# An encoder layer on one core: folded softmax sums, another load order and another place for the layer norm's root

## The chip, the cores and the metric

The kernel runs on one core of one Trainium2 chip. A core has five engines with queues of their own: TensorE (PE in the profile, PEld for its weight loads), VectorE (DVE), ScalarE (ACT), GpSimd (POOL) and SyncE (SP), which only issues DMAs here. The metric is the device time of one execution in microseconds (us). Times inside an execution count from the start of its profiled span.

## The reference

One encoder layer on 2048 tokens of width 1024. A projection of `x` feeds two groups of heads: gated linear attention (group A) and softmax attention with compressed queries and keys (group B). Their outputs stand side by side, go through one output projection, and a residual with layer norm follows. What the change touches:

```python
# group B: 4 heads, blocks of queries
s = einsum('bqhd,bkhd->bhqk', qn, k_nope) + einsum('bqhr,bkr->bhqk', qr, k_r)
p = softmax(s, axis=-1)
o_b = einsum('bhqk,bkhv->bqhv', p, v) * silu(gate)
# both groups
mixed = concatenate([o_a, o_b], axis=-1) @ w_out
# layer norm of the residual
r = DEEPNORM_ALPHA * x + mixed
mu, var = mean(r), mean((r - mu) ** 2)          # along the width of 1024
out = (r - mu) * rsqrt(var + 1e-5) * ln_g + ln_b
```

All tensors are float32. The kernel splits each operand of a product into a high and a low part and multiplies three times (`mm3`, L417: lines L419 to L421), so that the faster matmul format keeps enough digits.

## The kernel before

Two sweeps over chunks of 128 tokens make the projections and group A and leave the compressed keys, values and rotary keys of group B on the chip. Then comes `attention` (L1499), which holds both the softmax attention and the output stage.

**Attention.** There are 16 blocks (`nb`): for each of four query blocks of 512 columns, four heads. A block has eight steps (`NP`) of two key tiles each. Scores stand with keys on the partitions and the 512 queries along the free axis. One step issues ten score matmuls (`scores`), a copy to SBUF on ACT (`copy`, L1542), maxima on DVE (`smax`, L1555); once the block's maximum is known (`tmax`, `rmax`, `bmax`: transposes, a reduce, transposes back) a subtraction on DVE (`sub`, L1579), the exponential (`exp`, L1583) and the high part (`phi`) on ACT, the low part on POOL (`plo`, L371) and six matmuls with the values (`pv`).

The denominators are sums of the exponentials over all keys. DVE adds four of the eight steps in a PSUM bank `ap` (`acc0` on ACT copies the first half step, L1598; `acc`, L1606), POOL adds the other four into an SBUF tile `as` of two halves (printed as `acc`). `tot` joins them: `ap` plus one half, then that plus the other half, into SBUF (L1629, L1630). `tsum` turns the 128x512 sum with four transposes (L1642), `rcp` reduces over the 128 partial sums and takes reciprocals (L1648, L1649), a column of 128x4. `keep` (L1654) stores it from ACT's queue, in 512 pieces of four bytes, into `r_s`, from where the output stage reads it along rows. For the last block `turn` transposes the column to 4x128 instead and `rows` (L1666, L1667) copies it on ACT and stores it from SP's queue. `oh` and `ol` split the block's output on ACT and DVE, `y` multiplies it by the value weights, `yc` copies and stores it (L1689, L1690).

**Order.** Each of these steps has a place, in units of a step (`PLACE`, L74; for the last block `PLACE_LAST`, L96; for what is already of the output stage `PLACE_OUT`, L107). A list of all steps sorted by place fixes the order of the instructions on every engine, SP's queue included (L1761). The place of a step is its block's first step plus what the table says; `tot` and what follows it count from the block's last step (L1726). Tiles of the pools `pX` (tag `x`) and `pA` (tag `ap`), each one PSUM bank, and the tile `as` have one buffer: who writes the next waits for all who used the last.

**Output stage.** `OutProj` works through 16 chunks of 128 tokens. `load` (L1863 to L1866) brings a chunk of both groups' outputs (`of`) and of gate and reciprocals (`gr`), `gate` (L1872, POOL) multiplies, `hi` and `lo` split on ACT and POOL, `load_res` (L1885) brings the residual `xr` into one of three buffers. `part` multiplies one eighth of the width for the two halves of the columns. Weight blocks come through `fetch_w` (L1829), which has one buffer, and `split_hi`, `split_lo`. `residual` adds `xr` on DVE (L1939) and collects statistics (L1940); `finish` (L1942) makes mean and variance, subtracts and scales (L1951), takes the root and writes (L1954, L1955). The root is `rsqrt` (L444): logarithm and exponential on ACT (L432, L433) for a first value, one Newton step in four small DVE operations (L438 to L441).

Chunks 0 to 3 start within the sorted list. For chunks 4 to 15 (L1799) the order is written out for ACT, POOL and SP only: splits of chunk c+2, loads of chunk c+4, residual load of chunk c+1, product, finish. In that loop chunk 4 also issues `keep` of block 14 and the last block's `tot`, `oh`, `ol`; chunk 5 its `tsum` and `rcp`; chunk 7 `turn`, `y`, `rows`, `yc`. Even chunks from 2 on use the banks `mb` and `x` (`pmb`, `px` in the profile), the others a pair of banks `pS` (`po`).

Of the kernel before, what the change touches and what calls it, by code (L numbers as in the profile page):

```python
# [9 lines left out]
F32 = mybir.dt.float32  # L10
F32R = mybir.dt.float32r
I32 = mybir.dt.int32
AF = mybir.ActivationFunctionType
ALU = mybir.AluOpType
AX = mybir.AxisListType
# [3 lines left out]
P = 128  # L19
# [3 lines left out]
NCH = S // P  # L23
# [4 lines left out]
QB = 512  # L28
# [56 lines left out]
    rmax=1.27,  # L85
    bmax=1.48,
    tot=11.2,
    tsum=12.04,
    rcp=13.55,
    keep=14.21,  # L90
    oh=12.34,
    ol=12.99,
    y=16.55,
    yc=16.9,
# [20 lines left out]
    w_hi=0.74,  # L115
    w_step=6.49,
    w_lo=4.26,
    part=(1.05, 2.03, 5.45, 8.05, 10.24, 17.37, 21.96, 27.24),
    whole=(24.99, 55.73),
    sum=(38.16, 49.19),  # L120
# [234 lines left out]
class K:  # L355
# [80 lines left out]
    def rsqrt_b(self, u, y, t, w, r):  # L436
# [3 lines left out]
        nc.vector.tensor_scalar(t, w, -0.5, 1.5, ALU.mult, ALU.add)  # L440
        nc.vector.tensor_tensor(r, t, y, ALU.mult)  # L441
        return r

    def rsqrt(self, pool, u, n, name):  # L444
        return self.rsqrt_b(*self.rsqrt_a(pool, u, n, name))


    def load_w(self, pool, stage, src, ncols, tag, k, lo_eng="dve", hi_eng="act", bufs=None):
# [1050 lines left out]
    def attention(self):  # L1499
        tc, nc = self.tc, self.nc  # L1500
        mm = nc.tensor.matmul
        V, G, Ac = nc.vector, nc.gpsimd, nc.scalar
        NP = NKT // 2
        with ExitStack() as ctx:
# [4 lines left out]
            pM, pO, pX, pA, pS = bank("pM"), bank("pO"), bank("pX"), bank("pA"), bank("pS", 2)  # L1509
            blocks = [(h, b) for b in range(NQB) for h in range(H)]  # L1510
            nb = len(blocks)
            stt = [dict(s=[None] * NP) for _ in blocks]
# [110 lines left out]
            def tot(i):  # L1623
                d = stt[i]
                if i == nb - 1:
                    d["as"] = self.keep.tile([P, 2, QB], F32, tag="acc", name=f"acc{i}")
                    V.tensor_copy(d["as"][:, 0], d["ap"])
                    return
                V.tensor_tensor(d["ap"], d["ap"], d["as"][:, 1], ALU.add)  # L1629
                V.tensor_tensor(d["as"][:, 0], d["ap"], d["as"][:, 0], ALU.add)  # L1630

            def close(i, shape, name, other):


                p, tag = other if i == nb - 1 else (pX, "x")
                return p.tile(shape, F32, tag=tag, name=name)

            def tsum(i):
                d = stt[i]
                d["x"] = close(i, [P, 4, P], f"sx{i}", (pA, "ap"))  # L1640
                for e in range(4):
                    nc.tensor.transpose(d["x"][:, e], d["as"][:, 0, e * P:(e + 1) * P], self.ident)  # L1642

            def rcp(i):

                d = stt[i]
                rc = op.sm.tile([P, 4], F32, tag="rc", name=f"rc{i}")
                V.tensor_reduce(rc, d["x"], AX.X, ALU.add)  # L1648
                V.reciprocal(rc, rc)  # L1649
                d["rc"] = rc  # L1650

            def keep(i):
                h, b = blocks[i]
                Ac.dma_start(self.r_s[b][:, h].rearrange("o (e p) -> p (o e)", p=P), stt[i]["rc"])  # L1654

            def turn(i):

                d = stt[i]
                t = pA.tile([P, QB], F32, tag="ap", name=f"rt{i}")
                nc.tensor.transpose(t[0:4, 0:P], d["rc"], self.ident)  # L1660
                d["rt"] = t[0:4, 0:P]

# [38 lines left out]
            op = OutProj(self, ctx, qp, bp, sp, pS, pM, pX, pO, pA)  # L1701
            first = [dict(c=c) for c in range(4)]
# [4 lines left out]
            def put(place, fn, *a):  # L1707
                todo.append((place, len(todo), fn, a))

            def at(f, i, j=None):  # L1710
                p = PLACE_LAST.get(f, PLACE[f]) if i == nb - 1 else PLACE[f]
                return p[j] if isinstance(p, tuple) else p

            own = (("tot", tot), ("tsum", tsum), ("rcp", rcp), ("keep", keep), ("oh", oh), ("ol", ol), ("y", y), ("yc", yc))
            own_late = tuple(e for e in own if e[1] is not keep)
            for i in range(nb):
                for j in range(NP):
                    t = NP * i + j
# [11 lines left out]
            out = PLACE_OUT  # L1730
            end = NP * nb
            for k in range(NK):
                if k < PRE_W:
                    v = NP * (PRE_BLOCK + k)
                    hi, lo = v + out["pre_hi"], v + out["pre_lo"]
                else:
                    hi = end + out["w_hi"] + (k - PRE_W) * out["w_step"]
                    lo = hi + out["w_lo"]
                if k == 0:
                    put(hi - 6, op.fetch_w, k)  # L1740
                put(hi, op.split_hi, k)
                put(lo, op.split_lo, k)
                if k + 1 < NK:
                    put(lo + 0.01, op.fetch_w, k + 1)
                else:
                    put(max(lo, end + 26) + 0.02, op.load_ln)
                put(end + out["part"][k], lambda k: [op.part(o, k) for o in first[:2]], k)
            for c, o in enumerate(first):
                put(end + (out["lo1"][c - 1] + 0.01 if c else out["hi0"][0] - 6), op.load, o)
                for j in range(2):  # L1750
# [16 lines left out]
            rest = {c: o for c, o in enumerate(first)}  # L1767

            def load(c):
                if c < NCH:  # L1770
                    rest[c] = dict(c=c)
                    op.load(rest[c])

            def split(c):
                if c < NCH:
                    op.hi(rest[c], 0)
                    op.lo(rest[c], 0)
                    op.gate(rest[c])
                    op.hi(rest[c], 1)
                    op.lo(rest[c], 1)  # L1780
# [17 lines left out]
                    op.finish(rest[c])  # L1798
            for c in range(4, NCH):  # L1799
                with fixed():  # L1800
                    split(c + 2)
                    load(c + 4)
                    if 4 < c < NCH - 1:
                        op.load_res(rest[c + 1])
                    op.product(rest[c])
                    op.finish(rest[c])
                with self.after(*last.values()), fixed():
                    if c == 4:
                        keep(nb - 2)
                    for f in {4: (tot, oh, ol), 5: (tsum, rcp), 7: (turn, y, rows, yc)}.get(c, ()):  # L1810
                        f(nb - 1)


class OutProj:
# [127 lines left out]
    def finish(self, o):  # L1942
        kern, nc, sm = self.k, self.nc, self.sm
        V, Ac = nc.vector, nc.scalar
        c, rr = o["c"], o["rr"]
        mv = sm.tile([P, 2], F32, tag="mv", name=f"mv{c}")
        u = sm.tile([P, 1], F32, tag="u", name=f"u{c}")
        V.bn_aggr(mv, o["bn"])
        V.tensor_scalar(u, mv[:, 1:2], LN_EPS, None, ALU.add)
        for n in range(2):  # L1950
            V.scalar_tensor_tensor(rr[:, n], rr[:, n], mv[:, 0:1], self.ln[0][:, n], ALU.subtract, ALU.mult)  # L1951
        rs = kern.rsqrt(sm, u, 1, f"ln{c}")
        for n in range(2):
            V.scalar_tensor_tensor(rr[:, n], rr[:, n], rs, self.ln[1][:, n], ALU.mult, ALU.add)  # L1954
            nc.sync.dma_start(kern.out[c * P:(c + 1) * P, n * 512:(n + 1) * 512], rr[:, n])  # L1955
# [68 lines left out]
```

## Time and profile before

| | us |
|---|---|
| median of 3 runs | 1300.88 |
| lowest and highest | 1297.87, 1301.57 |
| profiled execution | 1303.84 |
| its span | 1301.6 |
| mean granted TensorE clock | 0.996 of full speed |

Attention runs from about 627 us to 1110, the output stage from there to the end; the two overlap for some 20 us. A row of a timeline has start, duration, engine, line, operation, `out<-in` by the program's names, shape and count; in brackets stands how long the engine had been idle and what released it. Operations of one kind that follow each other are merged into one row.

### The profile page before, as it was taken

How to read it: one execution, taken by the hardware profiler on the slowest of the kernel's cores; microseconds unless marked ns; L12 is line 12 of the kernel's file. 1: busy time of each engine (PE TensorE's matmuls, PEld its weight loads, DVE VectorE, ACT ScalarE, POOL GpSimd, SP SyncE). 2: the span in 40 equal slices, each digit the busy share in tenths (PEclk: the TensorE clock that was granted, in tenths of full speed). 3: DMA queues.
4: the chain of work that ended last, by engine and by line, in shares of the span. 5: the costliest groups of instructions: out<-in, count | busy, mean ns of one | idle time of the engine just before them, and what ended most of it. 6: DMA issues, size and time to landing. Idle time of an engine off the chain costs nothing.

```text
span 1301.6 us, 19963 instructions
## 1 busy us (share of the span) xinstructions
PE 1273.0 (98%) x7017; PEld 1122.8 (86%) x7017; DVE 927.6 (71%) x1712; ACT 817.4 (63%) x1387; POOL 785.4 (60%) x500
## 2 busy tenths in 40 slices
PE   7999999999999999999999999999999999998997
PEld 7999999999889999999788888888888888886886
DVE  6865664545665555555888888888888888386998
ACT  7765556565676566555788887888888887411110
POOL 0244232332567666661398888889999999934441
PEclk9999999999999999999999999999999999999999
DMA  8232222131566555656301112212233110376563
GB/s 288 72 90 66 81 66 81 53 94 53 200 203 192 187 179 200 206 179 203 96 1 41 42 41 50 52 46 57 57 89 90 41 41 25 121 241 163 189 203 102
DMA packets 113964, 145.82 MB, mean 112 GB/s; under 512 B 18018, under 2 KB 70630, under 8 KB 113864
## 3 DMA queue, kind: packets, MB, share of 16 engines
q1 hardware_dynamic: 105176, 142.41, 35.6%
q0 software_dynamic: 768, 2.10, 0.4%
q8 instruction: 56, 0.92, 0.3%
q10 hardware_dynamic: 7920, 0.03, 0.3%
q14 instruction: 44, 0.36, 0.1%
HBM read 94.14 MB, written 50.36 MB: 111 GB/s over the span
## 4 chain that ended last, share of the span: by engine, by line
PE 83%; DMA 4%; DVE 3%; ACT 3%; POOL 2%; issue 2%; SPq 0%; DVEq 0%; POOLq 0%; ACTq 0%
PE o L419 4%; PE o L420 4%; PE pS L1533 4%; PE o L421 4%; PE pS L1535 4%; PE pS L1536 4%; PE pS L1537 4%; PE pS L1534 4%; PE ipa L419 4%; PE ipa L421 3%; PE ipa L420 3%; PE pz L420 2%; PE pz L419 2%; PE pz L421 2%; PE ipg L419 2%; PE ipg L420 2%
## 5 line engine op out<-in xcount | busy, mean ns | idle before, releaser
L371 POOL TENSOR_TENSOR pl<-s,ph 128x1024 fp32r<-128x1024 f32 x128 | 306.4, 2413 | 58.4 <-ACT ph L365 54.6
L1555 DVE TENSOR_TENSOR rm<-pS,rm 128x512 f32<-128x512 f32 x210 | 144.9, 690 | 36.6 <-ACT s L1542 31.5
L1542 ACT ACTIVATE s<-pS 128x1024 f32<-128x1024 f32 x128 | 131.5, 1027 | 60.8 <-PE pS L1537 52.3
L1579 DVE TENSOR_TENSOR s<-s,mb 128x1024 f32<-128x1024 f32 x128 | 151.2, 1213 | 9.1 <-PE mb L1573 9.0
L1042 POOL TENSOR_TENSOR Us<-Us,cw 128x512 f32<-128x512 f32 x16 | 18.6, 1162 | 212.4 <-DVE Us L1040 180.7
L365 ACT ACTIVATE ph<-s 128x1024 fp32r<-128x1024 f32 x128 | 135.1, 1057 | 17.1 <-PE o L421 16.6
L1583 ACT ACTIVATE s<-s 128x1024 f32<-128x1024 f32 x128 | 131.4, 1050 | 13.4 <-DVE s L1579 13.3
L419 PE MATMUL ipa<-wah,xah 128*128 128x384 f32 (+1 forms) x384 | 131.2, 342 | 6.9 <-ACT wah L365 6.4
L420 PE MATMUL ipa<-wal,xah 128*128 128x384 f32 (+1 forms) x384 | 125.5, 327 | 0.1
L421 PE MATMUL ipa<-wah,xal 128*128 128x384 f32 (+1 forms) x384 | 124.8, 325 | 0.0
L1533 PE MATMUL pS<-qh,ckvT_h 128*128 128x512 f32 x256 | 102.5, 400 | 0.8 <-ACT s L1583 0.4
L419 PE MATMUL o<-ph,vh 128*128 128x512 f32 x256 | 101.0, 395 | 0.0
L421 PE MATMUL o<-ph,vl 128*128 128x512 f32 x256 | 99.8, 390 | 0.0
L1536 PE MATMUL pS<-rh,krs 128*128 128x512 f32 x256 | 99.8, 390 | 0.0
L1535 PE MATMUL pS<-qh,ckvT_l 128*128 128x512 f32 x256 | 99.8, 390 | 0.0
L1537 PE MATMUL pS<-rl,krs 128*128 128x512 f32 x256 | 99.7, 389 | 0.0
L1534 PE MATMUL pS<-ql,ckvT_h 128*128 128x512 f32 x256 | 99.7, 389 | 0.0
L420 PE MATMUL o<-pl,vh 128*128 128x512 f32 x256 | 99.7, 389 | 0.0
L371 POOL TENSOR_TENSOR ol<-of,oh 128x512 fp32r<-128x512 f32 x32 | 42.9, 1343 | 70.4 <-ACT oh L365 69.6
L1606 DVE TENSOR_TENSOR ap<-ap,s 128x512 f32<-128x512 f32 x120 | 83.1, 692 | 2.6 <-ACT s L1583 0.7
L419 PEld LDWEIGHTS ipa<-wah,xah 128*128 128x128 f32 x384 | 72.9, 190 | 9.9 <-ACT wah L365 6.6
L419 PE MATMUL pz<-xch,wzh 128*128 128x256 f32 x256 | 74.8, 292 | 0.0
(325 smaller groups left out, 3825.2 us busy)
## 6 DMA issues: line engine op xcount, KB each, us to landing
xcf<-xT_dram SPq DMA_DIRECT2D x16, 512.0 KB, 4.5
xr<-x_dram SPq DMA_DIRECT2D x16, 512.0 KB, 5.7
out_dram<-rr SPq DMA_DIRECT2D x32, 256.0 KB, 2.4
xaf<-xT_dram SPq DMA_DIRECT2D x14, 512.0 KB, 3.8
oib<-oi_s SPq DMA_DIRECT2D x16, 256.0 KB, 3.9
qdb<-qd_s SPq DMA_DIRECT2D x16, 256.0 KB, 5.0
SU<-su_s SPq DMA_DIRECT2D x16, 256.0 KB, 4.4
ub<-u_s SPq DMA_DIRECT2D x16, 256.0 KB, 4.2
```

What stands on the lines that cost most here:

```text
L365: return nc.scalar.activation(dst, src, AF.Copy).ins
L371: return e.tensor_tensor(dst, src, hi.bitcast(F32), ALU.subtract).ins
L419: mm(out, ah, bh, start=start, stop=False)
L420: mm(out, ah, bl, start=False, stop=False)
L421: mm(out, al, bh, start=False, stop=stop)
L1533: mm(ps[:, e], kh, qh, start=True, stop=False)
L1534: mm(ps[:, e], kh, ql, start=False, stop=False)
L1535: mm(ps[:, e], kl, qh, start=False, stop=False)
L1536: mm(ps[:, e], kr, rh, start=False, stop=False)
L1537: mm(ps[:, e], kr, rl, start=False, stop=True)
L1555: V.tensor_tensor(d["rm"], src[:, e], d["rm"], ALU.max)
L1579: V.tensor_tensor(s, s, d["mb"][:, None, :].to_broadcast([P, 2, QB]), ALU.subtract)
```

## The change

It makes five edits.

1. **Folded sum, blocks 0 to 14.** `tot` adds both halves of `as` into the PSUM bank. Two ACT copies (`own_half`) take, of query columns 0 to 255, the sums on partitions 0 to 63, and of columns 256 to 511 those on partitions 64 to 127, into one 128x256 tile. Two DVE additions (`fold`) add what stands on the other 64 partitions. `tsum` then needs two transposes and `rcp` reduces 64 sums for each query instead of 128. Block 15 keeps the old way.
2. **Block 14's reciprocals.** `keep` in the output stage is gone. `turn` (in bank `pX`) and `rows` of block 14 stand in the sorted list at 13.6 and 13.65, after its `rcp`.
3. **First products of the output stage.** Chunk 0's first `part` moves ahead of the last block's `tmax` (place 0.255 past the end instead of 1.05); chunk 1's stays.
4. **Load order.** From chunk 5 on `load_res` of the next chunk is issued ahead of the splits and the four loads.
5. **The layer norm's root.** The four small DVE operations become four ACT copies with factor and addend.

```diff
 PLACE = dict(
     tot=11.2,
-    tsum=12.04,
+    half=11.7,
+    fold=11.95,
+    tsum=12.37,
     rcp=13.55,
     keep=14.21,
+    turn=13.6,
+    rows=13.65,
...
 PLACE_OUT = dict(
+    part0=(0.255, 1.05),
     part=(1.05, 2.03, 5.45, 8.05, 10.24, 17.37, 21.96, 27.24),
...
             def tot(i):
...
-                V.tensor_tensor(d["ap"], d["ap"], d["as"][:, 1], ALU.add)
-                V.tensor_tensor(d["as"][:, 0], d["ap"], d["as"][:, 0], ALU.add)
+                for e in range(2):
+                    V.tensor_tensor(d["ap"], d["ap"], d["as"][:, e], ALU.add)
+
+            halves = [(slice(64 * e, 64 * e + 64), slice(64 - 64 * e, 128 - 64 * e), slice(e * QB // 2, (e + 1) * QB // 2))
+                      for e in range(2)]
+
+            def own_half(i):
+                d = stt[i]
+                for own_p, _, qs in halves:
+                    Ac.activation(d["as"][own_p, 0, :QB // 2], d["ap"][own_p, qs], AF.Copy)
+
+            def fold(i):
+                d = stt[i]
+                for own_p, other_p, qs in halves:
+                    h = d["as"][own_p, 0, :QB // 2]
+                    V.tensor_tensor(h, d["ap"][other_p, qs], h, ALU.add)
...
             def tsum(i):
-                for e in range(4):
+                for e in range(4 if i == nb - 1 else 2):
                     nc.tensor.transpose(d["x"][:, e], d["as"][:, 0, e * P:(e + 1) * P], self.ident)
...
             def rcp(i):
-                V.tensor_reduce(rc, d["x"], AX.X, ALU.add)
+                if i == nb - 1:
+                    V.tensor_reduce(rc, d["x"], AX.X, ALU.add)
+                else:
+                    V.tensor_reduce(rc.rearrange("p (e j) -> p j e", e=2),
+                                    d["x"][:, 0:2].rearrange("p j (e k) -> p j e k", e=2), AX.X, ALU.add)
...
             def turn(i):
-                t = pA.tile([P, QB], F32, tag="ap", name=f"rt{i}")
+                t = (pA if i == nb - 1 else pX).tile([P, QB], F32, tag="ap" if i == nb - 1 else "x", name=f"rt{i}")
...
-            own = (("tot", tot), ("tsum", tsum), ("rcp", rcp), ("keep", keep), ("oh", oh), ("ol", ol), ("y", y), ("yc", yc))
-            own_late = tuple(e for e in own if e[1] is not keep)
+            own = (("tot", tot), ("half", own_half), ("fold", fold), ("tsum", tsum), ("rcp", rcp), ("keep", keep), ("oh", oh), ("ol", ol), ("y", y), ("yc", yc))
+            own_late = tuple(e for e in own if e[1] is not keep) + (("turn", turn), ("rows", rows))
...
-                put(end + out["part"][k], lambda k: [op.part(o, k) for o in first[:2]], k)
+                for o, place in zip(first, out["part0"]):
+                    put(end + (out["part"][k] if k else place), op.part, o, k)
...
             for c in range(4, NCH):
                 with fixed():
+                    if 4 < c < NCH - 1:
+                        op.load_res(rest[c + 1])
                     split(c + 2)
                     load(c + 4)
-                    if 4 < c < NCH - 1:
-                        op.load_res(rest[c + 1])
                     op.product(rest[c])
                     op.finish(rest[c])
                 with self.after(*last.values()), fixed():
-                    if c == 4:
-                        keep(nb - 2)
...
     def finish(self, o):
-        rs = kern.rsqrt(sm, u, 1, f"ln{c}")
+        l, y, t, w, rs = (sm.tile([P, 1], F32, tag=f"rs_{i}", name=f"ln{c}_{i}") for i in "lytwr")
+        Ac.activation(l, u, AF.Ln)
+        Ac.activation(y, l, AF.Exp, scale=-0.5)
+        Ac.activation(t, y, AF.Copy, scale=y)
+        Ac.activation(w, t, AF.Copy, scale=u)
+        Ac.activation(t, w, AF.Copy, scale=-0.5, bias=1.5)
+        Ac.activation(rs, t, AF.Copy, scale=y)
```

More of the change, by code (lines that the diff above doesn't have):

```diff
@@ L442, in rsqrt_b @@
         return r
-    def rsqrt(self, pool, u, n, name):
-        return self.rsqrt_b(*self.rsqrt_a(pool, u, n, name))
     def load_w(self, pool, stage, src, ncols, tag, k, lo_eng="dve", hi_eng="act", bufs=None):
```

## The prediction

> **What bounds the kernel now.** I read the page's busy times first, then the busy time by stretches for attention and output, then the timelines of TensorE (PE), VectorE (DVE), ScalarE (ACT), GpSimd (POOL) and SyncE's queue (SP) where PE stands still. The stretches' columns are length, busy time and count of PE, weight load, DVE, ACT and POOL, granted clock, DMA share, GB/s.
>
> ```profile
> PE 1273.0 (98%) x7017; PEld 1122.8 (86%) x7017; DVE 927.6 (71%) x1712; ACT 817.4 (63%) x1387; POOL 785.4 (60%) x500
> 627.00:1090.00 463.00, 461.07 (x2116) 380.81 (x2115) 402.61 (x535) 381.85 (x410) 406.87 (x177) 1.00 0.18 48
> 1190.00:1210.00 20.00, 14.72 (x58) 11.59 (x57) 8.23 (x14) 2.19 (x5) 7.79 (x7) 0.83 0.83 239
> 1230.00:1250.00 20.00, 20.00 (x90) 16.57 (x89) 19.55 (x28) 3.13 (x8) 9.22 (x8) 1.00 0.66 205
> ```
>
> PE is full almost everywhere: 461 of 463 us in attention, 20 of 20 in the settled output stage, where DVE (19.55) is close behind. So an edit is worth what it takes from PE's own work or from PE's pauses. The one large pause lies between 1190 and 1210, and the clock falls there too.
>
> **The folded sum, on PE.**
>
> ```profile
> 950.47 0.39 PE L1537 MATMUL pS<-rl,krs 128*128 128x512 f32 x1
> 950.70 0.60 PE L1642 MATMUL sx<-ident,acc 128*128 128x128 f32 x4
> 951.37 0.39 PE L1534 MATMUL pS<-ql,ckvT_h 128*128 128x512 f32 x1
> 954.78 0.39 PE L1533 MATMUL pS<-qh,ckvT_h 128*128 128x512 f32 x1
> ```
>
> A 128x512 matmul takes 0.23 of PE's time (950.47 to 950.70). The four transposes and one matmul take 0.67 (950.70 to 951.37), so four cost 0.44, and two less save 0.22 a block. Fourteen blocks give 14 x 0.22 = 3.1 us; block 14 is counted below, and block 15 keeps its four.
>
> **The folded sum, on ACT and DVE.** It adds two 64x256 copies on ACT and two 64x256 adds on DVE; the reduce is halved.
>
> ```profile
> 944.19 0.69 DVE L1630 TENSOR_TENSOR acc<-ap,acc 128x512 f32<-128x512 f32 x1
> 946.12 1.21 DVE L1579 TENSOR_TENSOR s<-s,mb 128x1024 f32<-128x1024 f32 x1
> 947.25 1.41 DVE L1555 TENSOR_TENSOR rm<-pS,rm 128x512 f32<-128x512 f32 x2
> 952.02 1.42 DVE L1555 TENSOR_TENSOR rm<-pS,rm 128x512 f32<-128x512 f32 x2 [0.50 <-ACT s L1542]
> 945.97 1.03 ACT L1542 ACTIVATE s<-pS 128x1024 f32<-128x1024 f32 x1 [0.56 <-PE pS L1537]
> 946.89 0.59 ACT L1598 ACTIVATE ap<-s 128x512 f32<-128x512 f32 x1
> 950.96 1.03 ACT L1542 ACTIVATE s<-pS 128x1024 f32<-128x1024 f32 x1 [0.78 <-PE pS L1537]
> L1689 ACT ACTIVATE yc<-y 128x512 f32<-128x512 f32 x16 | 9.4, 589 | 0.0
> L1666 ACT ACTIVATE rt<-rt 4x128 f32<-4x128 f32 x1 | 0.2, 250 | 0.0
> L1930 DVE SCALAR_TENSOR_TENSOR rr<-xr,po 128x256 f32<-128x256 f32 x1 | 0.4, 404 | 0.0
> ```
>
> No row shows a 64x256 copy; between 0.25 (128 elements a partition) and 0.59 (512) I take 0.37, nearer to the small one by its 256 elements. The add I take at the 0.40 of a 128x256 operation. ACT is free at 945.41 (0.56 before 945.97) and the total is done at 944.88, so both copies are over by about 946.1, in the time in which ACT waited. The fold stands in DVE's order between the subtraction (to 947.3) and the maxima (now from 947.25): 0.7 us, to 948.0.
>
> Here is the new wait. The sum tile has one buffer, and the next block's first copy into it (L1598) is placed before the previous block's fold. It must wait for the fold: from 946.89 to 948.03, 1.14 later. Queued behind it on ACT are an exponential, two splits and the copy of 950.96. That copy had 0.78 to spare, and the two shortened gaps leave it some 0.1 late. The maxima that follow it ended at 953.44 and PE wants their bank at 954.78, so 1.34 more is spare. The sum says that PE loses nothing, and that it starts to lose beyond 0.78 + 1.34 = 2.1 us of delay at L1598.
>
> **The end of attention.**
>
> ```profile
> 1091.60 0.63 PE L1561 MATMUL mx<-ident,rm 128*128 128x128 f32 x4 [0.68 <-DVE rm L1555]
> 1103.49 0.60 PE L1642 MATMUL sx<-ident,acc 128*128 128x128 f32 x4
> 1104.32 0.69 DVE L371 TENSOR_TENSOR ofl<-o,ofh 128x512 fp32r<-128x512 f32 x1 [2.44 <-ACT ofh L365]
> 1104.93 0.68 DVE L1648 TENSOR_REDUCE rc<-sx 128x4 f32<-128x512 f32 x1
> 1105.64 0.18 DVE L1649 RECIPROCAL rc<-rc 128x4 f32<-128x4 f32 x1
> 1101.68 0.33 SPq L1829 DMA_DIRECT2D wof<-wO_dram  x1
> 1107.03 1.05 ACT L365 ACTIVATE woh<-wof 128x1024 fp32r<-128x1024 f32 x1
> 1108.62 2.42 POOL L371 TENSOR_TENSOR wol<-wof,woh 128x1024 fp32r<-128x1024 f32 x1
> 1116.87 0.39 PE L419 MATMUL po<-woh,oh 128*128 128x512 f32 x1
> ```
>
> Moving chunk 0's first product ahead of the maximum's transposes fills the pause before 1091.60 with work that PE does later anyway: the last matmul before it leaves about 0.8 us, and with the slow restart I take 0.9. PE then reaches block 14's transposes at 1102.6 instead of 1103.49.
>
> The turn of block 14 costs more. PE's written order has nothing between these transposes (place 131.37) and the turn (132.6); the next product stands at 133.45. The turn needs the reciprocal, which on DVE stands behind the split of the output, which waits for ACT. Before, the reciprocal ended at 1105.82 while PE worked on from 1103.94. Now ACT comes to that split only after the awaited L1598 and one exponential, by my count 0.1 later than for the 1104.32 here, and the half reduce saves 0.28: 1105.6. PE stands from 1102.8 to 1105.65 and resumes, after the transpose, at 1105.95 where it was at 1103.94: **2.0 us lost**, block 14's two transposes and the filled pause included. At best only transposes, reduce and reciprocal lie between (0.9 us of pause, nothing lost); at worst one more subtraction (1.21) comes first on DVE.
>
> The row's DMA is queued on SP ahead of the fetch of weight block 5 and holds it from 1101.68 to about 1106.4, 4.7 later. From that fetch to the split on ACT at 1107.03 passed 5.35; held up by no more than that, the split ends by 1112.8 and POOL's (2.42) by 1115.3. PE wants it at 1116.87 + 2.0. Hidden, by 3.6 us.
>
> **The output stage.**
>
> ```profile
> 1178.04 0.39 ACTq L1654 DMA_DIRECT2D r_s<-rc  x1
> DMA to landing us min/median/max: 9.2/11.0/13.7
> 1184.00:1188.00 4.00, 4.00 (x19) 3.33 (x18) 4.00 (x11) 0.24 (x1) 1.62 (x1) 1.00 0.38 31
> SPq L1864 <- DMA r_s<-rc: 5.5, 1, 5.5
> 1194.76 0.70 SPq L1885 DMA_DIRECT2D xr<-x_dram  x1
> 1203.02 0.69 DVE L1939 SCALAR_TENSOR_TENSOR rr<-xr,pmb 128x512 f32<-128x512 f32 x1 [11.53 <-DMA xr<-x_dram]
> 1198.18 0.40 PE L421 MATMUL y<-ofh,wv_l 128*128 128x512 f32 x1
> 1203.86 0.77 PE L419 MATMUL pmb<-woh,oh 128*128 128x512 f32 x1 [5.28 <-DVE rr L1939]
> 1201.00:1202.00 1.00, 0.00 (x0) 0.00 (x0) 0.00 (x0) 0.00 (x0) 0.00 (x0) 0.58 0.92 305
> 1204.00:1208.00 4.00, 4.00 (x10) 3.14 (x11) 3.90 (x8) 0.93 (x3) 0.74 (x1) 0.50 0.81 235
> ```
>
> Read it backwards. PE waited 5.28 us for a bank, which DVE frees when chunk 6's residual has come; that load was issued at 1194.76, behind chunk 9's four loads, and one of these sat 5.5 us for the store of block 14's reciprocals, issued by ACT at 1178.04 and landing 13.7 us later. From 1201 to 1208 the clock was at half: by the 0.58 of 1201 to 1202 it fell about 2.6 us into the pause. Without the pause PE goes on at 1198.41, and the ten matmuls done by 1208.15 (0.43 apart) take 2.3: 9.74 - 2.27 = **7.5 us**.
>
> The change removes both causes: the store goes out during block 15, turned into rows, and chunk 6's load stands first, right behind chunk 4's output, by about 1185.2. It then lands near 1192 even at the 7.8 us that it took here. DVE has been idle since 1191.5 (11.53 before 1203.02). PE wants the bank at 1198.41, so next in line is PE's own work, with 6 us to spare; if that cover goes, the loss returns us for us.
>
> The fall after 2.6 us bears on the turn's 2.9 us too. [...]
>
> The root on ACT takes four small operations from DVE and puts four on ACT, which has 3.13 busy of 20. DVE was not what PE waited for in 1230 to 1250, so this is worth nothing until the last chunk:
>
> ```profile
> 1294.85 0.20 ACT L432 ACTIVATE ln_l<-u 128x1 f32<-128x1 f32 x1 [8.38 <-DVE u L1949]
> 1295.08 0.20 ACT L433 ACTIVATE ln_y<-ln_l 128x1 f32<-128x1 f32 x1
> 1296.82 1.41 DVE L1954 SCALAR_TENSOR_TENSOR rr<-rr,ln_r,lnb 128x512 f32<-128x512 f32 x2
> ```
>
> Dependent small operations start 0.23 apart on ACT; with a column as factor I allow 0.32. The four after Exp start at 1295.31 and take 0.9 to 1.3, and L1954 starts 0.2 to 0.6 earlier: I take 0.3.
>
> **Sum.** 3.1 - 2.0 + 7.5 + 0.3 = 8.9 us less. The profiled execution took 1303.84 (its span 1301.6 and 2.2 around it), 2.96 above the median of 1300.88. I put that excess into the pause: its store landed after 13.7, the median store after 11.0, and 2.7 less pause is about the difference. So I take 1303.84 - 8.9 = **1295**, not 1292, which it would be if the excess were spread over the kernel. About 0.3% (3.9 us) is what a measurement here can tell from no change: faster is below 1297.0, slower above 1304.8.
>
> **Rivals.** *The turn's pause brings the clock down.* One stretch of 3.4 us at half speed, half of the 6.8 seen here, costs 1.7: 1296.7. For it, the fall 2.6 us into a pause; against it, the pause before 1091.60 (0.68) left the clock alone (1.00 over 627 to 1090 and 0.63 for the four transposes, near the 0.60 of other blocks), so somewhere between lies a limit that 2.9 may or may not pass. Chance 0.17.
>
> *The output pause only moves.* Were chunk 6's load late for another reason, a slot freed late or a crowded queue (DMA share 0.83 in 1190 to 1210), the 7.5 would stay: 1.4 gained, 1299.5 from the median, no change. For it: the loads are crowded; against: while the store was under way, DMA moved only 31 GB/s at 1184 to 1188, so it has room once the store is gone. Chance 0.13.
>
> *The fold holds up ACT.* If copies and adds cost what the 128x1024 forms cost (1.03 and 1.21), the copies end at 947.4, the fold at 949.7, and L1598 comes 2.9 late: 0.8 beyond what is spare, in 15 blocks 11.6 us: 1306.6, slower. It decides from 2.1 us on. For it: ACT, DVE and POOL are each over four fifths busy in attention; against it: a quarter of the elements. Chance 0.12.
>
> **How the numbers follow.** The forecast holds with 0.56, its own range 1291 to 1297; 0.02 is left for a gain beyond it. Faster: 0.55 + 0.09 of the clock case + 0.02 = 0.66. Same: 0.01 + 0.08 + 0.13 = 0.22. Slower: 0.12. The range 1290.5 to 1300.5 takes in the clock, the moved pause and both bounds of the turn, and leaves out the fold.
>
> **What would show it.** Right: two transposes in sx, blocks 0.22 apart less, L1598 starting about a microsecond later with no PE wait on scores; a PE pause near 3 us before rt; no wait of pmb on rr after 1150; the root's four lines gone from DVE. Wrong: a repeating PE wait on ACT's copies, a pause of pmb that stays, or a clock below 1.00 after rt.

## The result and the profile after

The changed kernel took 1297.54 us (median of 19 runs, 1295.85 to 1299.18) beside 1301.18 for the kernel before (19 runs, 1297.87 to 1303.84): a ratio of 0.9973, with an interval of 0.9966 to 0.998. It is 3.6 us faster. The interval leaves out 1, but 0.28% is inside the 0.3% that the prediction set as its bound, so by that bound the change counts as no change, by a hair. The forecast was 1295.0 with a range of 1290.5 to 1300.5: the time is 2.5 above the one and inside the other.

The profiled execution took 1299.13 (span 1296.9) where that of before took 1303.84 (span 1301.6): 4.7 less. To see where these 4.7 lie, three instructions serve as landmarks: block 0's maximum transposes (attention starts), the first matmul of pmb (chunk 2's product, just behind the end of attention), and the last matmul of the kernel. First the timeline of PE of the kernel before, then that of the changed kernel; the columns are start, duration, engine, line, operation.

```profile
630.62 0.66 PE L1561 MATMUL mx<-ident,rm 128*128 128x128 f32 x4 [0.31 <-DVE rm L1555]
1125.03 0.39 PE L419 MATMUL pmb<-woh,oh 128*128 128x512 f32 x1
1293.15 0.28 PE L421 MATMUL pap<-woh,ol 128*128 128x256 f32 x1
```

```profile
632.47 0.66 PE L1563 MATMUL mx<-ident,rm 128*128 128x128 f32 x4 [0.31 <-DVE rm L1557]
1128.10 0.39 PE L424 MATMUL pmb<-woh,oh 128*128 128x512 f32 x1
1288.74 0.28 PE L426 MATMUL pap<-woh,ol 128*128 128x256 f32 x1
```

| stretch | before | after | difference | predicted |
| --- | --- | --- | --- | --- |
| start to attention, to the first mx | 630.62 | 632.47 | +1.85 | 0 |
| A: first mx to the first pmb | 494.41 | 495.63 | +1.22 | -1.1 |
| B: first pmb to the last matmul | 168.12 | 160.64 | -7.48 | -7.5 |
| last matmul to the end of the span | 8.45 | 8.16 | -0.29 | -0.3 |

(A's predicted -1.1 is the -3.1 of the transposes and the +2.0 of the turn.) B and the tail came out to a few hundredths. The first stretch holds nothing that was changed; in the thirteen profiles of this study it lies between 630.50 and 633.74, so its 1.85 is a difference between executions. What failed is A, by 2.3 us.

The page and the stretches of the changed kernel, with the columns of the prediction's:

```profile
PE 1270.2 (98%) x6988; PEld 1119.6 (86%) x6988; DVE 908.5 (70%) x1678; ACT 842.7 (65%) x1482; POOL 790.9 (61%) x500
627.00:1090.00 463.00, 461.08 (x2101) 380.24 (x2100) 413.23 (x567) 391.18 (x440) 406.64 (x177) 1.00 0.18 48
1106.25:1106.50 0.25, 0.25 (x2) 0.20 (x2) 0.25 (x1) 0.25 (x1) 0.00 (x0) 0.88 0.00 0
1107.00:1108.00 1.00, 1.00 (x4) 0.76 (x3) 0.98 (x2) 0.75 (x1) 1.00 (x1) 0.50 0.60 205
1109.75:1110.00 0.25, 0.25 (x3) 0.21 (x2) 0.25 (x2) 0.25 (x1) 0.00 (x0) 0.79 0.00 0
1230.00:1250.00 20.00, 20.00 (x90) 16.55 (x89) 11.67 (x20) 4.95 (x16) 9.90 (x8) 1.00 0.63 199
```

In attention PE is as full as before (461.08 of 463), so the folded sum added no wait that repeats; DVE has 10.6 more there and ACT 9.3, hidden. In the settled output stage DVE fell from 19.55 of 20 to 11.67 and PE, full before and after, gained nothing by it. The new thing is the clock: between 1106.25 and 1110 it stood at half. A quarter with 0.88 was at full speed for 0.76 of its time, so the clock fell at 1106.44, and by the same reckoning it rose at 1109.85: 3.41 us.

The end of attention, from the timelines of PE, ACT, DVE and SP's queue:

```profile
1099.51 0.77 ACT L1640 ACTIVATE acc<-ap 64x256 f32<-64x256 f32 x2 [0.46 <-DVE ap L1632]
1100.61 0.86 DVE L1646 TENSOR_TENSOR acc<-ap,acc 64x256 f32<-64x256 f32 x2
1101.56 0.60 ACT L1600 ACTIVATE ap<-s 128x512 f32<-128x512 f32 x1 [1.28 <-DVE acc L1646]
1101.62 0.40 PE L1658 MATMUL sx<-ident,acc 128*128 128x128 f32 x2
1103.90 0.69 DVE L376 TENSOR_TENSOR ofl<-o,ofh 128x512 fp32r<-128x512 f32 x1 [1.00 <-ACT ofh L370]
1104.51 0.41 DVE L1667 TENSOR_REDUCE rc<-sx 128x4 f32<-128x256 f32 x1
1104.96 0.18 DVE L1669 RECIPROCAL rc<-rc 128x4 f32<-128x4 f32 x1
1105.28 0.27 PE L1680 MATMUL rt<-ident,rc 128*4 128x128 f32 x1 [3.26 <-DVE rc L1669]
1105.62 0.39 PE L425 MATMUL po<-wol,oh 128*128 128x512 f32 x1
1106.24 0.35 SPq L1848 DMA_DIRECT2D wof<-wO_dram  x1
```

Read the 3.26 backwards: the turn waits for the reciprocal, this for the split of the output, this for ACT, and ACT was kept 1.28 at L1600 by the fold. PE's last work before it ended at 1102.0. The fetch of weight block 5 went out at 1106.24, as worked out.

In the output stage, the load of chunk 6's residual and its use:

```profile
1185.26 0.45 SPq L1904 DMA_DIRECT2D xr<-x_dram  x1
1191.87 0.68 DVE L1958 SCALAR_TENSOR_TENSOR rr<-xr,pmb 128x512 f32<-128x512 f32 x1
1201.48 0.39 PE L424 MATMUL pmb<-woh,oh 128*128 128x512 f32 x1
```

The load went out 9.5 us earlier, DVE didn't wait for it, and PE takes the bank without a wait. The list of PE's waits holds only the turn behind 1080 us.

### The profile page after: what moved, and what is told of

It is laid out like the page before. It is cut to its first block, busy times and chain, and to the rows that moved or that the text cites. A ratio compares the mean times of both kernels' runs of the same rounds, so it can differ in the third digit from the quotient of the medians.

```text
span 1296.9 us, 19995 instructions
## 1 busy us (share of the span) xinstructions
PE 1270.2 (98%) x6988; PEld 1119.6 (86%) x6988; DVE 908.5 (70%) x1678; ACT 842.7 (65%) x1482; POOL 790.9 (61%) x500
## 4 chain that ended last, share of the span: by engine, by line
PE 86%; ACT 3%; DVE 2%; POOL 2%; issue 2%; DMA 1%; SPq 0%; DVEq 0%; ACTq 0%; POOLq 0%
PE o L424 4%; PE o L426 4%; PE pS L1535 4%; PE o L425 4%; PE pS L1537 4%; PE pS L1536 4%; PE pS L1538 4%; PE pS L1539 4%; PE ipa L424 4%; PE ipa L426 3%; PE ipa L425 3%; PE po L426 2%; PE po L425 2%; PE po L424 2%; PE pz L425 2%; PE pz L426 2%
```

## The experiments

Theory A: the gain that is missing went into the turn of block 14, as a pause of 3.26 and a half clock of 3.41 (3.41 / 2 = 1.7 lost). Theory B: the turn costs little in most executions, and the pause of the output stage was smaller in most of them than in the profiled one. The two aren't exclusive, so the experiments also take the change apart. "Before" in each ratio is the kernel before, run on the same chip beside it. The table of A and B for all of them stands at the end of this section, read off the same three rows. The runs come from several chips, on which the kernel before had medians of 1301.18 to 1303.13, so medians of different experiments are compared with care, and the ratios and A and B are the better measure.

**The turn later.** Base: the changed kernel.

```
-    turn=13.6,
-    rows=13.65,
+    turn=14.6,
+    rows=14.65,
```

> The changed kernel with the turn of block 14 and its row's store moved by 1.0 place, behind the product of weight block 2 (places 14.6 and 14.65 instead of 13.6 and 13.65). Theory A (the gain that is missing went into the pause of 3.26 us before the turn and the half clock behind it, about 1.65): part k2 (12 matmuls at 0.23, 2.8 us) now stands between block 14's two sum transposes and the turn, the pause shrinks to at most 0.5, the clock stays at 1.00 from 1106 to 1110, and the time falls by 4 to 4.6 us, to about 1293.2. Theory B (the turn is cheap in most executions, and the missing gain is a pause of the output stage that was smaller in most executions of the kernel before than in the profiled one): only what the profiled execution shows as pause can come back, without the clock: 1294.5 or more. Theory C (a wait takes its place: the sum bank is released later, y of block 14 comes late): the pause moves to before y and the time stays at 1297.5.

Measured: 1293.85 (1293.59 to 1295.43), ratio 0.9943 (0.9929 to 0.9956). PE's timeline of this kernel:

```profile
1103.57 0.27 PE L1680 MATMUL rt<-ident,rc 128*4 128x128 f32 x1 [0.49 <-DVE rc L1669]
1104.25 0.50 PE L424 MATMUL y<-ofh,wv_h 128*128 128x512 f32 x1 [0.41 <-ACT rt L1686]
```

The pause shrank from 3.26 to 0.49, a second one of 0.41 came before y, the clock stayed at 1.00, and 3.7 us came back. Theory C's wait exists, but at 0.41. A is 3.63 shorter (495.63 to 492.00), B is unchanged; Theory A holds. Beyond the profiles, the mean granted clock of the executions points the same way: 0.995 to 0.998, in the middle 0.997, in the 19 of the changed kernel, and 0.998 or 0.999 in the five with the late turn; 3.41 us at half speed are worth 0.0013. This is weak evidence: the mean also counts the half clock behind the last matmul, 4.9 us in the profile of before and 2.7 in that of the changed kernel, and the changed kernel's profiled execution, with the fall in it, has 0.998 as well.

**The turn undone.** Base: the changed kernel.

```
-    own_late = ... + (("turn", turn), ("rows", rows))
+    own_late = ...
                 with self.after(*last.values()), fixed():
+                    if c == 4:
+                        keep(nb - 2)
```

> The changed kernel without the turn of block 14; its reciprocals are stored as before, by ScalarE's queue in 4-byte pieces at the start of the output stage. Load order as changed. Theory A with the load order as what removes the output pause: no pause at the turn, none in the output stage, 1297.5 - 4.9 = 1292.6. Theory A with the store as what makes the output pause: the turn's 4.9 come back, but chunk 6's load or chunk 9's loads are late again and PE waits some 5 us in 1195 to 1205: 1297 to 1298. Theory B: turn cheap, order enough: 1296 to 1297.5.

Measured: 1293.54 (1292.41 to 1296.15), ratio 0.994 (0.9926 to 0.9953). A is 491.37, B 160.61: with the new load order PE doesn't wait although the 4-byte store is back. The first case of Theory A, 0.9 off. By the ratios, the other edits without the turn save 7.8 us; with it 3.5. The use of chunk 6's residual, on DVE, and of the bank, on PE:

```profile
1197.16 0.69 DVE L1960 SCALAR_TENSOR_TENSOR rr<-xr,pmb 128x512 f32<-128x512 f32 x1 [9.44 <-DMA xr<-x_dram]
1198.46 0.39 PE L424 MATMUL pmb<-woh,oh 128*128 128x512 f32 x1
```

The load was late again, but the bank came free at 1197.85, 0.6 before PE wanted it.

**The load order alone.** Base: the kernel before.

```
                 with fixed():
+                    if 4 < c < NCH - 1:
+                        op.load_res(rest[c + 1])
                     split(c + 2)
                     load(c + 4)
-                    if 4 < c < NCH - 1:
-                        op.load_res(rest[c + 1])
```

> The kernel before with one edit, chunk c+1's residual load ahead of the split and the loads of chunk c+2 and c+4. The store of block 14's reciprocals stays. If the order is what counts: chunk 6's load is issued near 1185 instead of 1194.8, no wait of pmb on rr, the half clock gone, 7.5 us less in the profiled execution and 4.5 to 7.5 less than the median of 1301.2: 1294 to 1296.7. If the store is what counts (it takes 9 to 14 us to land and holds whatever lies behind it): the wait moves to another tile of chunk 8 or 9 and the time stays within 1 us of 1301.2.

Measured: 1296.81 (1296.26 to 1297.22), ratio 0.9962 (0.9949 to 0.9974). SP's queue, DVE and PE:

```profile
1185.65 0.45 SPq L1885 DMA_DIRECT2D xr<-x_dram  x1
SPq L1863 <- DMA r_s<-rc: 4.1, 1, 4.1
1197.63 0.69 DVE L1939 SCALAR_TENSOR_TENSOR rr<-xr,pmb 128x512 f32<-128x512 f32 x1 [4.66 <-DMA xr<-x_dram]
1198.88 0.39 PE L419 MATMUL pmb<-woh,oh 128*128 128x512 f32 x1
```

B fell from 168.12 to 160.64, the whole 7.48. It is close, though: SP's queue still waits 4.1 for the store, now with the next chunk's load; chunk 6's load, issued at 1185.65, let DVE start only at 1197.63, 12 us later, and the bank came free at 1198.32 where PE wanted it at 1198.88. The order alone removes the pause with half a microsecond to spare. In the changed kernel, without the store, it is 1192.55 against 1201.48.

**The folded sum alone.** Base: the kernel before, with the copies, the fold, the two transposes and the half reduce in blocks 0 to 14 (`half`, `fold`, `tsum=12.37` as in the change).

> The kernel before with the folded sum alone (blocks 0 to 14: copies of own halves, fold, two transposes, half reduce). By the blocks' period: 15 x 0.22 = 3.3 us less, 1297.9, and the output stage as before, its pause of pmb on rr included (this profile shows how long that is in another execution: Theory B says clearly below 5.28, Theory A about the same). Rival: the copies and adds cost part of it again at the end of attention, where ACT and DVE are late: 1299 to 1300.

Measured: 1297.48 (1296.97 to 1297.93), ratio 0.9967 (0.9954 to 0.9979), 0.4 below the expected 1297.9. A is 491.49, 2.92 less than before. Its output stage still has the pause:

```profile
SPq L1884 <- DMA r_s<-rc: 3.0, 1, 3.0
1190.28 0.73 SPq L1905 DMA_DIRECT2D xr<-x_dram  x1
1198.13 0.47 PE L421 MATMUL pmb<-woh,oh 128*128 128x512 f32 x1 [2.25 <-DVE rr L1959]
1198.50:1198.75 0.25, 0.25 (x3) 0.15 (x2) 0.25 (x2) 0.00 (x0) 0.00 (x0) 0.64 1.14 350
1201.75:1202.00 0.25, 0.25 (x2) 0.25 (x1) 0.25 (x2) 0.00 (x0) 0.25 (x1) 0.53 1.13 410
```

2.25 where before had 5.28, and 3.41 us of half clock (1198.57 to 1201.98) where before had 6.83: 4.08 us of B instead of 7.48. Theory B is right that the pause varies: by 3.03 between these two profiles, which is more than the folded sum is worth.

**The turn alone.** Base: the kernel before (the turn's bank as in the change).

```
+    turn=13.6,
+    rows=13.65,
+            own_late = ... + (("turn", turn), ("rows", rows))
-                    if c == 4:
-                        keep(nb - 2)
```

> The kernel before with one edit: block 14's reciprocals turned and stored as a row in block 15 (places 13.6 and 13.65), no 4-byte store in the output stage; load order, sums and root as before. If removing the store is enough: no pause of pmb on rr although the load order is the old one, worth the 4.9 that the load order alone gave against 1302.1; against it a pause of about 2 us before the turn (no folded sum, chunk 0's first product not moved, so PE comes there about a microsecond later than in the changed kernel), and 1.7 if the clock falls after it as it did after the 2.3 us of the kernel with the folded sum alone: 1301.0 with the fall, 1299.4 without. If the old load order keeps the pause by itself, chunk 6's load stands behind chunk 9's four loads and lands after 1198: 1304 or more.

Measured: 1299.15 (1298.29 to 1301.08), ratio 0.9972 (0.9962 to 0.9982). PE's timeline, two quarters and SP's queue:

```profile
1106.91 0.27 PE L1662 MATMUL rt<-ident,rc 128*4 128x128 f32 x1 [1.88 <-DVE rc L1651]
1108.25:1108.50 0.25, 0.25 (x2) 0.17 (x1) 0.25 (x1) 0.25 (x2) 0.00 (x0) 0.54 0.03 6
1111.50:1111.75 0.25, 0.25 (x2) 0.24 (x1) 0.25 (x1) 0.25 (x1) 0.00 (x0) 0.63 0.00 0
1192.73 0.62 SPq L1885 DMA_DIRECT2D xr<-x_dram  x1
```

B is 160.64 here too, with the load in its old place behind chunk 9's loads. So either edit alone removes the pause; together they pay for it twice, and only the turn has a price: A is 498.48, 4.07 more than before, of which 1.88 is the pause and 1.7 the half clock after it. By the profile it is the expected case with the fall; the median is 1.9 below the 1301.0 given for that case (this profile's own execution took 1301.08, with the median at 1299.15). The mean granted clock of the nine executions goes from 0.996 (the profiled one) to 0.999, 0.003 where 3.41 us at half speed are 0.0013; so the fall may be missing in some, but no profile shows it.

**Chunk 0's first product put back.** Base: the kernel with the late turn; `part0=(1.05, 1.05)`.

> The kernel with the late turn (1293.85), with chunk 0's first product put back beside chunk 1's. Where PE is the bound again, the pause before block 15's maximum transposes comes back: 0.7 to 0.9 more, 1294.7. If the turn and y of block 14 still wait for the reciprocals, these 0.7 only shorten that wait (0.5 + 0.4 are left of it): no change within 0.3.

Measured: 1294.04 (1293.32 to 1294.84), ratio 0.9933 (0.9921 to 0.9944). A is 492.03 against 492.00. The pause of 0.68 before the maximum transposes is back, and the 0.49 before the turn is gone: the edit fills a pause that a later wait for the same chain gives back. The +0.9 of the prediction is worth nothing while the turn waits.

**The root back on VectorE.** Base: the kernel with the late turn.

```
-        l, y, t, w, rs = (...)
-        Ac.activation(l, u, AF.Ln)
...
+        rs = kern.rsqrt(sm, u, 1, f"ln{c}")
```

> The kernel with the late turn (1293.85), with the layer norm's root back on VectorE. Theory A: only the last chunk counts, 0.28 more by the trace, 1294.1, and PE shows no wait for VectorE in the output stage although that is busy 19.5 of 20 us there again. Rival: VectorE at 19.5 of 20 frees banks late and PE waits for pmb or px in several chunks: 1295.5 or more.

Measured: 1295.45 (1294.71 to 1297.32), ratio 0.9945 (0.9933 to 0.9957), 1.4 above the kernel with chunk 0's product put back (1294.04), run on the same chip. The profile shows 0.24 of that: A 491.96, B 160.64 as with the root on ACT, no wait of PE for DVE in the output stage, and 8.48 from the last matmul to the end where the late turn has 8.24. In its profile attention starts at 632.12, where the late turn's has 630.76, ahead of everything that was edited. Theory A by the profile; the median is beside the rival's 1295.5, but the rival's sign, PE waiting for pmb or px, isn't there. Why the median is more than a microsecond higher stays open.

**Turn and y later still.** Base: the kernel with the late turn; turn, rows and y of block 14 at 17.12, 17.14 and 17.16 (yc at 17.5).

> The kernel with the late turn, with the turn, its row's store and y of block 14 behind the product of weight block 3 as well (places 17.12, 17.14 and 17.16). Theory A: the two waits that are left (0.5 before the turn, 0.4 before y) go, 0.9 less: 1293.0. Rival: the sum bank is held longer, or a later product waits for its input instead: 1293.8 or more.

Measured: 1293.88 (1292.63 to 1295.72), ratio 0.9931 (0.9919 to 0.9944). The rival: A is 0.44 shorter, but in B, at 1178.53, PE waits 0.62 for a split by POOL, and B is 1.26 longer (the other 0.6 shows no single wait). No gain over the late turn.

**The two kernels again**, each for a second profile.

> The kernel before, unchanged, for a second profile. The first profile had its store land after 13.7 us and a pause of 5.28 us with two stretches of half clock; the kernel with the folded sum alone had 11.3, 2.25 and one stretch. If the size of the pause follows the landing of the store, a landing near 11 us leaves a pause of 2 to 3 us, one stretch of 3.4 us at half clock and from the first maximum transposes of attention to the last matmul about 3 us less than the 662.5 of the first profile. If the pause belongs to the load order alone, it is again above 5 whatever the store takes.

> The changed kernel, unchanged, for a second profile. If the pause before the turn brings the clock down nearly always (the four pauses of 1.88 to 5.28 us seen so far were all followed by it), there is again a pause of 3.2 to 3.4 us and one stretch of 3.4 us at half clock behind it, and from the first maximum transposes to the last matmul 656.3 within 0.4. [...]

Measured: 1304.32 and 1298.28. Kernel before, second profile:

```profile
SPq L1864 <- DMA r_s<-rc: 3.6, 1, 3.6
1195.25 0.68 SPq L1885 DMA_DIRECT2D xr<-x_dram  x1
1203.41 0.76 PE L419 MATMUL pmb<-woh,oh 128*128 128x512 f32 x1 [3.83 <-DVE rr L1939]
1202.50:1202.75 0.25, 0.00 (x0) 0.00 (x0) 0.17 (x1) 0.00 (x0) 0.00 (x0) 0.72 0.87 324
1209.25:1209.50 0.25, 0.25 (x3) 0.18 (x2) 0.22 (x2) 0.00 (x0) 0.19 (x1) 0.62 0.08 33
```

Changed kernel, second profile:

```profile
1104.43 0.27 PE L1680 MATMUL rt<-ident,rc 128*4 128x128 f32 x1 [3.26 <-DVE rc L1669]
1105.75:1106.00 0.25, 0.25 (x3) 0.16 (x2) 0.25 (x1) 0.25 (x2) 0.00 (x0) 0.71 0.03 8
1109.25:1109.50 0.25, 0.25 (x2) 0.20 (x2) 0.25 (x1) 0.25 (x1) 0.00 (x0) 0.97 0.00 0
```

The changed kernel repeats itself: the same 3.26, again 3.41 of half clock (1105.86 to 1109.27), 656.25 for A and B together where the first profile had 656.27. The kernel before does not: its store landed after 11.8 us instead of 13.7 and the pause was 3.83 instead of 5.28, as the first case says. But the 3 us that were to go did not: the half clock is 6.83 long again (1202.61 to 1209.44), and as the pause was shorter, more of it fell on work. Before: 5.28 of pause and half of the 4.1 from 1203.86 to 1208, 7.4. Again: 3.83 and half of the 6.0 from 1203.41 to 1209.44, 6.8. So in these profiles the pause grew with the landing of the store: 13.7, 11.8 and 11.3 us of landing go with 5.5, 3.6 and 3.0 of SP's wait and 5.28, 3.83 and 2.25 of PE's. SP's wait followed the landing closely, PE's pause only in order, since the load's own time and the moment at which PE wanted the bank differed too. The half clock didn't shrink with the pause: 6.83, 6.83 and 3.41.

**Half a turn.** Base: the late turn with `part0=(1.05, 1.05)`.

```
-  put(end + (out["part"][k] if k else place), op.part, o, k)
+  put(end + (out["part"][k] + 0.3 * (k == 2 and o is first[1]) if k else place), op.part, o, k)
```

> The changed kernel with the turn between the two halves of weight block 2's product (chunk 0's six matmuls ahead of it, chunk 1's behind), and chunk 0's first product back beside chunk 1's: a pause before the turn of about 1.1 us, between the 0.7 that left the clock alone and the 1.9 that brought it down. If any pause over about a microsecond is enough, there is a stretch of 3.4 us at half clock behind it and the time is 1294.0 + 1.1 + 1.7 = 1296.8. If it takes half of a stretch of 3.4 us without work, the clock stays at 1.00 and the time is about 1294.7 to 1295.1.

Measured: 1295.06 (1294.18 to 1295.55), ratio 0.9943 (0.9927 to 0.996). PE's timeline and a stretch:

```profile
1103.24 0.27 PE L1680 MATMUL rt<-ident,rc 128*4 128x128 f32 x1 [0.71 <-DVE rc L1669]
1104.00:1108.00 4.00, 4.00 (x19) 3.29 (x19) 3.97 (x6) 3.20 (x4) 4.00 (x2) 1.00 0.18 66
```

The pause came out at 0.71, not 1.1, and the clock stayed. The time fits the case without the fall, but since the pause is no longer than those seen before, it only repeats that about 0.7 had no fall behind it; no pause between 0.79 and 1.88 was tried.

| kernel | median | A | B |
| --- | --- | --- | --- |
| before, two profiles | 1301.18 | 494.41, 494.71 | 168.12, 167.50 |
| after, two profiles | 1297.54 | 495.63, 495.65 | 160.64, 160.60 |
| late turn | 1293.85 | 492.00 | 160.60 |
| turn undone | 1293.54 | 491.37 | 160.61 |
| load order alone | 1296.81 | 494.41 | 160.64 |
| folded sum alone | 1297.48 | 491.49 | 164.72 |
| turn alone | 1299.15 | 498.48 | 160.64 |
| late turn, product back | 1294.04 | 492.03 | 160.69 |
| late turn, root on VectorE | 1295.45 | 491.96 | 160.64 |
| late turn, y later too | 1293.88 | 491.56 | 161.86 |
| half a turn | 1295.06 | 492.19 | 160.70 |

The parts add up. Folded sum -2.92 and turn +4.07 on 494.41 give 495.56; the changed kernel has 495.63.

## Why the prediction was right and wrong

**The folded sum (3.1) was right, and a little too high.** Alone it takes 2.92 off A, block 14 included. Block 0 to 13's sum transposes stand 31.10 us apart before, 30.89 in the changed kernel and 30.91 with the folded sum alone: 0.19 to 0.21 a block where 0.22 had been worked out. The two copies took 0.77, near the 0.37 apiece taken from neighbouring rows, the two adds 0.86 where 0.7 stood. L1600 waited 15.3 over fourteen blocks, 1.1 each as worked out (1.14), and 1.28 at the end of attention. PE waited 0.8 in all between 640 and 1080 us, and 0.4 before, so the rival of the held-up ACT, which needed 2.1, did not come about.

**The output stage (7.5) was right for the profiled execution**, 7.48 by B, and its cause is shown: the load order alone and the turn alone each give all of it. "The change removes both causes" was true and cost part of the gain: one would have done. The rival of the pause that only moves is out. Chunk 6's load landed 5.7 us after its issue, where 7.8 had been allowed; before, its reader had started 8.3 after the issue.

**The end of attention (2.0 lost) is the step that failed.** In A the turn and all that goes with it cost 495.63 - 494.41 + 3.1 = 4.3. Of the 2.3 that are missing, 1.7 is the half clock that followed the turn, the prediction's first rival, and the pause was 3.26 where 2.9 had been worked out. Of the 0.2 to 0.3 that are left, the folded sum's 2.92 for 3.1 covers most: with it the turn cost 4.1, as it did alone. The rival's 1296.7 is the nearest of the prediction's times to 1297.54. The flaw is in the weighing: the prediction had a row with a fall 2.6 us into a pause, and then gave the fall a chance of 0.17 and the sum without it 0.56. Against the fall it set the clock of 1.00 from 627 to 1090, a stretch that ends before the pause of 0.68 does. That the clock would stay up behind a pause of 2.9 was the author's estimate, and no run shows it: it fell after pauses of 1.88, 2.25 and 3.26 us. The slow restart in the 0.9 for the filled pause is small: the first matmul after a pause of 0.43 took 0.47 where the next took 0.40 (kernel before, 640.65 and 640.95).

**The end of the kernel (0.3) was right**: 0.29 in the tail, and PE shows no wait for DVE whether the root is on it or not. The last chunk's chain after:

```profile
1290.66 0.20 ACT L1973 ACTIVATE ln_y<-ln_l 128x1 f32<-128x1 f32 x1
1290.90 0.29 ACT L1974 ACTIVATE ln_t<-ln_y 128x1 f32<-128x1 f32 x1
1292.12 1.42 DVE L1979 SCALAR_TENSOR_TENSOR rr<-rr,ln_r,lnb 128x512 f32<-128x512 f32 x2 [0.40 <-ACT ln_r L1977]
```

A column as factor made the small operation 0.29 instead of 0.20.

**From the profile to the median.** The sum was made against 1303.84, with its excess of 2.96 over the median put into the pause. The load order alone gained 0.38% of 1302.14 in the medians (0.26 to 0.51), 4.9 us, where the profile has 7.48, so most of the excess does seem to belong there; a profile of an execution near 1301 with a smaller pause was not obtained, and the second one was again at the long end. With 4.9 for the pause, 2.9 for the folded sum, 0.3 for the end and 4.1 for the turn alone, the median should fall by 4.0; it fell by 3.6.

**A better version.** Folded sum, load order and root without the turn (1293.54, ratio 0.994), or with the turn one place later (1293.85, ratio 0.9943), are by A 4.3 and 3.6 us faster than the changed kernel, and by the ratios 7.8 and 7.4 faster than the one before. The two medians can't be told apart; the first, with the store still there, has 0.6 us of cover in the output stage; the second does without the store.

## What to carry to other kernels

Where two edits remove the same wait, price each of them alone: the second brings nothing and keeps its cost, and here the redundant one cost more than the folded sum saved. When an instruction that waits for another engine is put into the written order of the engine that sets the end, look for work that can stand in front of it; one place in the order was worth 3.7 us. Read the granted clock behind a pause of TensorE before pricing it: here the pauses of 1.88 to 3.26 us had 3.41 us of half clock behind them, 1.7 of loss, and those of 0.68 and 0.71 had none, so moving the turn one place gave back 3.7 where the pauses shrank by 2.4.

## What the runs showed of the hardware

In six profiles the granted clock fell to half between the start of attention and the last matmul, inside PE's longest pause or shortly after it:

| profile | pause, and its end | fall | rise | half clock |
| --- | --- | --- | --- | --- |
| before | 5.28, 1203.86 | 1201.17, inside | 1208.00 | 6.83 |
| before, second | 3.83, 1203.41 | 1202.61, inside | 1209.44 | 6.83 |
| folded sum alone | 2.25, 1198.13 | 1198.57, 0.44 after | 1201.98 | 3.41 |
| turn alone | 1.88, 1106.91 | 1108.27, 1.36 after | 1111.68 | 3.41 |
| after | 3.26, 1105.28 | 1106.44, 1.16 after | 1109.85 | 3.41 |
| after, second | 3.26, 1104.43 | 1105.86, 1.43 after | 1109.27 | 3.41 |

The four falls after a pause had 3.41 us of half clock behind them, the two inside a pause 6.83, of which PE stood the first 2.69 and 0.80. The pauses of 0.49 (late turn), 0.68 (load order alone) and 0.71 (half a turn), and one of 0.79 at the start of attention (after, 633.91), had a clock of 1.00 behind them.

The length of a standstill alone didn't set the fall. Behind the last matmul, which ends at 1293.43 in the kernel before and at 1289.02 in the changed one, the clock fell as follows:

```profile
1296.50:1296.75 0.25, 0.00 (x0) 0.00 (x0) 0.21 (x2) 0.00 (x0) 0.00 (x0) 0.99 0.00 0
```

```profile
1294.00:1294.25 0.25, 0.00 (x0) 0.00 (x0) 0.00 (x0) 0.00 (x0) 0.00 (x0) 0.85 1.06 385
```

That is at 1296.74, after 3.31 us without work, and at 1294.18, after 5.16, where with the turn alone a pause of 1.88 was followed by a fall (to some hundredths, since the ends of matmuls are modelled). What else decides isn't shown, nor what a pause between 0.79 and 1.88 does.

A load that went out while the store in 4-byte pieces was under way landed late, though it didn't wait for the store by name. Chunk 6's residual, 0.5 MB, let DVE, which waited for it, start 12.0 us after its issue with the load order alone and 15.3 with the turn undone (1181.87 to 1197.16), both with the store; without it, in the changed kernel, it landed after 5.7. It isn't a crowd of other loads: from 1186 to 1190 DMA moved 25 GB/s with the load order alone and 337 in the changed kernel. By what means the store holds the load isn't shown.
